# Attention layer of a two-layer decoder: the strided heads' O step six slots later, no weight or x read ahead of the last value rows, token sums in wider steps

## The chip, the cores and the metric

The kernel runs on one core of a Trainium2 chip. The metric is the device time of one execution in microseconds (us); the number given for a kernel is the median of several executions. Beside these times there is one execution taken by the hardware profiler: its time, its span (first to last recorded instruction) and its trace. The trace knows the engines PE (TensorE, matrix products), DVE (VectorE), ACT (ScalarE), POOL (GpSimd), SP (SyncE), and the DMA queues that these engines issue to; in rows of the trace `SPq` is a transfer issued on SP, `POOL ... DMA_DIRECT2D` one issued on POOL.

## What is computed

Two layers over 512 tokens of width 1024, all in float32. Layer 0 mixes tokens with dilated attention (8 output heads of width 128, three groups of heads whose windows and dilations are 128/1, 512/4 and 2048/16); layer 1 with a gated linear recurrence. Each mixer is followed by a convolutional FFN of inner width 3072. Only layer 0's mixer is touched here. Cut to what matters:

```
for layer in range(2):
    h = rms_norm(x, norm_mix_pre[layer])
    h = dilated_attention_mixer(h, w_qkv, w_o, rel_bias)      # layer 0
    x = x + rms_norm(h, norm_mix_post[layer])
    h = rms_norm(x, norm_ffn_pre[layer])
    h = conv_ffn(h, ...)
    x = x + rms_norm(h, norm_ffn_post[layer])

def dilated_attention_mixer(x, w_qkv, w_o, rel_bias):
    qkv = x @ w_qkv                       # 3 groups x (q, k, v) x 8 heads x 128
    for g in range(3):                    # per group: banded softmax attention over t, t-d, t-2d, ...
        o_g, lse_g = dilated_group_attention(q_g, k_g, v_g, bias_g, WINDOWS[g], DILATIONS[g])
    alpha = softmax(stack(lse), axis=0)   # the groups are mixed by their denominators
    return sum(alpha * o) @ w_o
```

## The kernel before

**Precision and weights.** Every operand of a large product is split into a high and a low part (`split`, lines 146 to 148: ACT writes the high part `whi` on L147, DVE the low part `wlo` on L148), and a product is three matmuls: high by high, low by high, high by low. Weights come from DRAM in chunks of 0.5 or 1 MB into `raw` tiles, of which there are `RAW_BUFS = 3`. `pump` (L275 to L309) splits the next piece of a chunk when there is room for it, and then starts chunk reads on SP (`load`, L317) as long as fewer than three are in hand. A read of chunk n+3 therefore waits for the DVE split that empties chunk n, and everything that SP is to issue after it waits too, since an engine works through its program in order.

**The order of the work.** PE's order is written out by slots. `slot(f, 0.25)` runs one piece of matmul work `f` (12 matmuls of a weight chain, or a quarter of a value tile) and then moves all the *sides*, generators that carry the vector work, the small products and the transfers of the heads, on by a quarter of their unit: a `yield 2` in a side is eight slots, a `yield 0.5` two. `later(n, f)` puts a piece n ticks later. There are no priorities at run time: each engine executes its own list in this order and waits on semaphores.

**The attention layer.** First come the 8 heads of the first group with the plain projections (head pairs `hp` 0 to 3, `local`), until about 157 us. At the same time `token_sums` (L818) forms sums and differences of the hidden state's token halves (`B` tiles, then their splits `T`) that the later chains use as operands; it is a side, and its steps were one tile apart in `yield 1`. Then follow four rounds of `ROUND = 44` slots, one for each pair of strided heads. A round holds four chains (queries and keys of the two other groups, L1171, with evictions and combinations on ACT and DVE in L1180 to L1189) and the value rows of the same heads (`value_quarters`, L1107).

**Value rows.** When a value tile of 128 tokens is done, `evict(t)` scales it on ACT (L1145) and writes it on SP to a DRAM array `vrows` (L1146). After the fourth, `by_residue` reads `vrows` back with a token stride of four into four tiles `vp` (L1203, SP), so that the dilated heads find their keys in one tile. In rounds 0 to 2 this is put five ticks after the last eviction; in round 3 right behind it.

**A strided head.** `strided(h)` scores (L1282), exponentiates, and sends the weights of its two groups to DRAM and back turned (`turned` L435, `fetches` L443, both on POOL, four reads to a fetch) into `ft`. It also sends its own mixing weights out and back as `cn` (L1317, L1319). After a pause (`yield 2`) comes the O step: 16 matmuls `O<-ft,vp` (L1348), a DVE product o*cn (L1351) and a DVE sum with the result in PSUM (L1354). The heads of `hp` start when their round's chains are done, so the O step of `hp` 0 falls into round 1, that of `hp` 1 into round 2, that of `hp` 2 into round 3. The last two heads, 6 and 7, come behind round 3 and turn their weights on PE instead (`PT`, L1337).

**Behind the rounds.** `rows_proj` multiplies by w_o (L392, `acc`). `prep(2)` does part of it ahead of the last heads' O step, `prep(4)` and `run` the rest, followed by the post norm (L555), the residual sum with x (L560), the pre norm of the FFN and its first matmuls (L392, `ps`). x has meanwhile lost its place in SBUF to the token sums; `x_again` reads it back in four transfers of 0.5 MB (L803, on POOL), and the two gain vectors are read on SP (L143). The chunks of the FFN's up projection (`raw<-in_ffn_w_up_dram`) are 1 MB each.

Of the kernel before, what the change touches and what calls it, by code (L numbers as in the profile page):

```python
# [81 lines left out]
def kernel(  # L82
# [65 lines left out]
        nc.vector.tensor_tensor(lo, raw, hi.bitcast(F32), op=ALU.subtract)  # L148

    plan = []  # L150
    state = {"dma": 0, "cv": 0, "used": 0, "live": 0, "next": 0, "hold": False, "even": False}
    raws, units, pieces = {}, {}, []
    sides, first_w, first_y, one = [], [], [], []

# [128 lines left out]
    def pump(limit=2):  # L283

        for _ in range(limit):
            if not pieces:
                refill()
            while pieces and pieces[0][0] is None:
                pieces.pop(0)[1]()
            if not pieces or pieces[0][0][0] >= state["dma"]:  # L290
                continue
            if state["live"] + 2 - (pieces[0][0][1] in HALF) <= HALVES:
                key, cuts, last = pieces.pop(0)
                cuts = cuts()
                his, los = [], []
                for n, raw in enumerate(cuts):
                    hi, lo = (
                        wp.tile([P] + list(raw.shape[1:]), F32R, tag=t, name=nm("w" + t)) for t in ("hi", "lo")
                    )
                    split(hi, lo, raw)  # L300
                    his.append(hi)
                    los.append(lo)
                units[key] = (his, los)
                state["live"] += len(cuts)
                state["used"] += last
                while pieces and pieces[0][0] is None:
                    pieces.pop(0)[1]()
            while state["dma"] < len(plan) and state["dma"] - state["used"] < RAW_BUFS:
                load()  # L309

    def load():
# [25 lines left out]
    def side(steps, delay=1):  # L337
        sides.append([delay, steps])
# [460 lines left out]
    def x_again():  # L799

        X[0] = cp.tile([P, 4, D], F32, tag="x_sb", name=nm("x_sb"))
        for t in range(4):
            nc.gpsimd.dma_start(X[0][:, t], x[0, t * P : (t + 1) * P, :])  # L803
        yield 0

    def x_back():

# [3 lines left out]
    def token_sums(hT, T, first=False):  # L811

        if not first:
            assert len(sides) == 1
            d = dp.tile([P, 4, D], F32, name=nm("x_kept"))
            nc.gpsimd.dma_start(d, X[0])
            kept.append(d)
        homes = cp.tile([P, 4, D], F32R, tag="x_sb", name=nm("T"))  # L818
        homes = [homes[:, n] for n in range(4)]
        homes += [cp.tile([P, D], F32R, tag="gain", name=nm("T"), bufs=2) for _ in range(1 if first else 2)]  # L820
        homes = [[h[:, 0:512], h[:, 512:1024]] for h in homes]
        if first:
            homes += [[gen(F32R, "T") for _ in range(2)]]
            homes += [[wp.tile([P, 512], F32R, tag=t, name=nm("T")) for _ in range(2)] for t in ("hi", "lo")]
            state["live"] += 2
        else:
            homes += [[gen(F32R, "T") for _ in range(2)] for _ in range(2)]
        homes = [[h.rearrange("p (k t) -> p k t", k=2) for h in hs] for hs in homes]
        yield 1

        def both(k0, n):
            o = gen(s="B").rearrange("p (k t) -> p k t", k=2)
            hi, lo = (h[:, k0 : k0 + 2, n * 256 : n * 256 + 256] for h in hT)
            tt(o, hi.bitcast(F32), lo.bitcast(F32), op=ALU.add)
            return o

        tt = nc.vector.tensor_tensor

        def negative(o, a, b):
            nc.vector.scalar_tensor_tensor(o, a, -1.0, b, op0=ALU.mult, op1=ALU.subtract)  # L840

        def whole(k0, n):
            return [both(k0 + 2 * k, n) for k in range(2)]

        def parted(n, b):
            for k in range(2):
                split(homes[2 * n][k], homes[2 * n + 1][k], b[k])

        b11, b12 = whole(0, 0), whole(0, 1)
        yield 1  # L850
        for k in range(2):
            tt(b11[k], b11[k], b12[k], op=ALU.subtract)
        parted(0, b11)
        yield 1
        b22 = whole(4, 1)
        for k in range(2):
            if first:
                tt(b12[k], b22[k], b12[k], op=ALU.subtract)
                negative(b22[k], b11[k], b22[k])
            else:  # L860
                tt(b12[k], b12[k], b22[k], op=ALU.subtract)
                tt(b22[k], b22[k], b11[k], op=ALU.add)
        yield 1
        parted(1, b22)
        T.extend([homes[2 * n], homes[2 * n + 1]] for n in range(4))
        yield 1 if first else 8
        parted(2, b12)
        yield 1 if first else 3
        b21 = whole(4, 0)
        yield 1  # L870
        for k in range(2):
            if first:
                negative(b21[k], b22[k], b21[k])
            else:
                tt(b21[k], b21[k], b22[k], op=ALU.subtract)
        yield 1
        parted(3, b21)

    LEFT = {5: ("s1", 1), 1: ("w11", 0), 3: ("s4", 1), 2: ("w12", 0), 6: ("s2", 1), 7: ("s3", 1), 4: ("a22", 1)}
# [104 lines left out]
    def attention(hT, post, pre):  # L984
# [142 lines left out]
        def value_quarters(vs, prep):  # L1127

            vd = dp.tile([S, 512], F32, name=f"vrows{len(vrows)}")
            vrows.append(vd)  # L1130
            ids = [chunk(), chunk()]
            banks = {}

            def quarter(t, u):
                if not u:
                    banks[t] = psum("v")
                products(banks[t], t, u, take(ids[u // 2], u % 2))
                if t == 3:
                    done()
                if u == 3:  # L1140
                    later(1, lambda: evict(t))

            def evict(t):
                o = gen(s="v")
                nc.scalar.activation(o, banks[t], AF.Copy, scale=first_y[0][:, t : t + 1])  # L1145
                nc.sync.dma_start(vd[t * P : (t + 1) * P, :], o)  # L1146
                if t == 3:
                    if prep:
                        by_residue(vd, vs)
                    else:  # L1150
                        later(5, lambda: by_residue(vd, vs))
                elif t == 2 and prep:
                    prep(2)

            order = [(t, u) for t in range(4) for u in range(4)]
            return [lambda t=t, u=u: quarter(t, u) for t, u in (order if prep else sorted(order, key=lambda x: x[1]))]
# [42 lines left out]
        def by_residue(vd, vs):  # L1199

            for r in range(4):
                o = gen(s="vp")
                nc.sync.dma_start(o, vd.rearrange("(u r) c -> r u c", r=4)[r])  # L1203
                vs.append(o)
# [68 lines left out]
        def strided(h, hh, qks, v):  # L1273
# [49 lines left out]
            if h < 6:  # L1323
                for d in ds:
                    pt, reads = fetches(d)
                    for read in reads:
                        read()
                        yield 0.5
                    pts.append(pt)
                yield 2  # L1330
            else:
                yield 1
                for L in Ls:
                    ps = psum("PT")
                    for r in range(4):
                        c = slice(r * P, (r + 1) * P)
                        nc.tensor.transpose(ps[:, c], L[:, c], ident)  # L1337
                    pt = gen(s="PT")
                    nc.scalar.activation(pt, ps, AF.Copy)
                    pts.append(pt.rearrange("p (r c) -> p r c", r=4))  # L1340
                if hh:
                    state["hold"] = False
                yield 4.25 if hh else 4.5
# [56 lines left out]
        for hp in range(4):  # L1400
            pairs, vs = [[[None] * 2 for _ in range(2)] for _ in range(2)], []
            for c in range(4):
                f = chain(right, pairs[c // 2][c % 2], None if c % 2 else SCALE)
                steps.update((ROUND * hp + APART * c + QUAD[p], f(p)) for p in QUAD)

            def heads(hp=hp, pairs=pairs, vs=vs):
                for hh in range(2):
                    side(strided(2 * hp + hh, hh, pairs, vs), 0.25 + 0.25 * hh)
                state["hold"] = True
                if hp == 3:  # L1410
                    side(x_again(), 6.25)

            end = ROUND * hp + max(QUAD.values()) + 3 * APART
            steps[end] = lambda f=steps[end], g=heads: (f(), later(2, g))
            steps.update((ROUND * hp + n, q) for n, q in zip(QUARTERS, value_quarters(vs, prep if hp == 3 else None)))
# [223 lines left out]
```

## Time and profile before

| | us |
|---|---|
| timed runs | 1456.08, 1457.62, 1460.43 |
| median of the timed runs | 1457.62 |
| profiled execution, its time | 1452.73 |
| profiled execution, its span | 1450.9 |
| PE busy in the span | 1426.5 |
| rounds 0 to 3 and the O step of the last heads | about 157 to 476 |

The profiled execution is 4.9 us shorter than the median of the timed ones; sums made on the trace stand against its own time. PE is the engine to read first: it is busy for 98% of the span, so time is won only where PE stands still or runs at a lower clock. In the trace's windows a column gives the clock that was granted to PE (1.00 is full speed, 0.50 half), another the share of the core's DMA engines in use (values a little over 1 occur).

### The profile page before, as it was taken

Reading aid. Unit: us, or ns where it says so; the run is one execution under the profiler, and the core shown is the slowest. Engines: PE = TensorE matmul, PEld = TensorE weight load, DVE = VectorE, ACT = ScalarE, POOL = GpSimd, SP = SyncE. Lnnn points to the kernel's source line nnn. Section 1 sums busy time; section 2 is a strip of 40 time slices with the busy share of each in tenths; the row PEclk is TensorE's granted clock in tenths of the full one; section 3 lists DMA queues with packets and bytes.
Section 4 is the critical chain, followed back from the end, with each engine's and each line's share of the span. In section 5 each row is a group of like instructions: output and inputs, shape, how many; then the busy total and the mean of one; then the engine's idle time right before and its main releaser. Section 6 shows DMA issues by size and latency. Waiting matters only on the chain.

```text
span 1450.9 us, 21582 instructions
## 1 busy us (share of the span) xinstructions
PE 1426.5 (98%) x8021; PEld 1250.4 (86%) x8021; DVE 1023.0 (71%) x2017; ACT 723.1 (50%) x1486; POOL 178.3 (12%) x313
## 2 busy tenths in 40 slices
PE   9999999999998999999999999999999999999998
PEld 7888999898986898899988888988898999988886
DVE  6685898786855789977774338868789977774333
ACT  7353556363635455555553334489564555553231
POOL 0241333030301100111000001000100111000000
PEclk9999999999999999999999999999999999999999
DMA  7553456464655535645453232441435645453201
GB/s 223 158 160 114 124 162 176 141 184 133 169 184 157 173 97 155 149 110 123 130 198 116 87 102 73 126 136 58 124 91 161 155 106 143 124 189 116 88 1 59
DMA packets 143266, 191.30 MB, mean 132 GB/s; under 512 B 9344, under 2 KB 119384, under 8 KB 142648
## 3 DMA queue, kind: packets, MB, share of 16 engines
q1 hardware_dynamic: 114280, 145.48, 31.4%
q0 software_dynamic: 28032, 43.39, 12.9%
q8 instruction: 63, 1.03, 0.3%
q10 hardware_dynamic: 848, 1.05, 0.2%
q14 instruction: 43, 0.35, 0.1%
HBM read 170.93 MB, written 18.96 MB: 131 GB/s over the span
## 4 chain that ended last, share of the span: by engine, by line
PE 63%; ACT 4%; DMA 3%; DVE 3%; issue 1%; POOL 0%; DVEq 0%; POOLq 0%; ACTq 0%; SPq 0%
PE ps L392 25%; PE acc L392 23%; PE ps L934 11%; PE v L1107 1%; DVE xb L1442 1%; PE ps L1171 1%; DMA vrows<-v 1%; ACT whi L147 1%; DVE wlo L148 1%; DMA crow<-s 1%; PE O L1348 1%; ACT sig L1463 1%; PE tr L482 1%; DMA ft<-turned 0%; ACT sig L1482 0%
## 5 line engine op out<-in xcount | busy, mean ns | idle before, releaser
L148 DVE TENSOR_TENSOR wlo<-raw,whi 128x512 fp32r<-128x512 f32 x600 | 395.7, 686 | 201.4 <-ACT whi L147 200.6
L147 ACT ACTIVATE whi<-raw 128x512 fp32r<-128x512 f32 x600 | 358.9, 627 | 312.1 <-PE acc L392 118.2
L392 PE MATMUL ps<-hT,whi 128*128 128x512 f32 (+1 forms) x1728 | 486.0, 367 | 0.0
L392 PEld LDWEIGHTS ps<-hT,whi 128*128 128x128 f32 x1728 | 308.2, 189 | 48.8
L392 PE MATMUL ps<-hT,wlo 128*128 128x512 f32 (+1 forms) x864 | 316.0, 366 | 0.0
L392 PE MATMUL acc<-whi,ahi 128*128 128x512 f32 x512 | 199.6, 390 | 0.0
L392 PE MATMUL acc<-whi,alo 128*128 128x512 f32 x512 | 199.4, 389 | 0.1
L392 PE MATMUL acc<-wlo,ahi 128*128 128x512 f32 x512 | 199.2, 389 | 0.0
L392 PEld LDWEIGHTS ps<-hT,wlo 128*128 128x128 f32 x864 | 163.0, 189 | 27.0
L753 DVE SCALAR_TENSOR_TENSOR u<-ps,cols,u 128x511 f32<-128x511 f32 x192 | 143.6, 748 | 49.0 <-ACT u L749 45.6
L749 ACT ACTIVATE u<-ps,cols 128x512 f32<-128x512 f32 x96 | 73.9, 770 | 82.6 <-DVE ps L949 42.0
L392 PEld LDWEIGHTS acc<-whi,alo 128*128 128x128 f32 x512 | 96.1, 188 | 20.3 <-DVE alo L148 0.5
L392 PEld LDWEIGHTS acc<-wlo,ahi 128*128 128x128 f32 x512 | 96.1, 188 | 20.0
L392 PEld LDWEIGHTS acc<-whi,ahi 128*128 128x128 f32 x512 | 96.1, 188 | 19.8
L1107 PE MATMUL v<-whi,hT 128*128 128x512 f32 x320 | 106.6, 396 | 0.0
L1171 PE MATMUL ps<-T,whi 128*128 128x256 f32 x512 | 93.2, 282 | 1.1 <-DVE ps L1189 1.1
L934 PE MATMUL ps<-T,whi 128*128 128x256 f32 x512 | 92.8, 280 | 0.0
L184 POOL DMA_DIRECT2D raw<-in_ffn_w_up_dram x32 | 41.4, 1453 | 361.8 <-DVE wlo L148 223.6
L1171 PEld LDWEIGHTS ps<-T,whi 128*128 128x128 f32 x512 | 79.7, 189 | 2.6 <-DVE ps L1189 1.6
L934 PEld LDWEIGHTS ps<-T,whi 128*128 128x128 f32 x512 | 80.1, 189 | 1.6
L443 POOL DMA_DIRECT2D ft<-turned x136 | 74.5, 555 | 32.0 <-issue 11.3
L1171 PE MATMUL ps<-hT,whi 128*128 128x256 f32 x384 | 72.2, 287 | 0.0
(212 smaller groups left out, 2021.6 us busy)
## 6 DMA issues: line engine op xcount, KB each, us to landing
raw<-in_ffn_w_up_dram SPq DMA_DIRECT2D x48, 1024.0 KB
raw<-in_attn_w_qkv_dram SPq DMA_DIRECT2D x67, 512.0 KB
raw<-in_ffn_w_down_dram SPq DMA_DIRECT2D x24, 1024.0 KB
raw<-in_ffn_w_up_dram POOLq DMA_DIRECT2D x32, 256.0 KB, 4.7
raw<-in_lru_w_in_dram SPq DMA_DIRECT2D x8, 1024.0 KB
turned<-T POOLq DMA_DIRECT2D x26, 256.0 KB, 3.2
ft<-turned POOLq DMA_DIRECT2D x104, 64.0 KB, 4.4
vrows<-v SPq DMA_DIRECT2D x16, 256.0 KB
```

The lines of the kernel that those rows point to most:

```text
L147: nc.scalar.activation(hi, raw, AF.Copy)
L148: nc.vector.tensor_tensor(lo, raw, hi.bitcast(F32), op=ALU.subtract)
L184: nc.gpsimd.dma_start(to, src, accum_op=ALU.add)
L392: mm(dst, l[a], r[b], start=start and n == 0, stop=stop and n == 2)
L443: nc.gpsimd.dma_start(t[32 * c : 32 * c + 32].rearrange("j (b x) -> j b x", b=4), d.rearrange("(b j) (c x) -> c j b x", j=32, c=4)[c],)
L482: nc.tensor.transpose(ps[:, k * P : (k + 1) * P], xs[i][:, k * P : (k + 1) * P], ident)
L749: nc.scalar.activation(u, ps, AF.Identity, scale=cc[:, j : j + 1], bias=cc[:, 48 + j : 49 + j])
L753: nc.vector.scalar_tensor_tensor(u[:, d:], ps[:, : S - d], wc, u[:, d:], op0=ALU.mult, op1=ALU.add)
L934: mm(y[b][:, 0:256], W[wa][0][:, k, :], right[n](ha, k), start=n in (1, 5) and k == q == 0, stop=k == 3 and q == 2, skip_group_check=True,)
L1107: mm(bank, hT[a][:, k, t * P : (t + 1) * P], W[b][k % 2][:, 0, :], start=(k, a, b) == (0, 0, 0), stop=(k, a, b) == (KD - 1, 1, 0),)
L1171: mm(dst, W[wa][0][:, k, :], right[n](ha, k), start=n in (1, 5) and k == q == 0, stop=k == 3 and q == 2, skip_group_check=True,)
L1348: mm(po[:, c], vtile(v, r, 2 * gi + hh), pts[gi][:, r], start=gi == 0, stop=gi == 1)
```

## The change

1. In `strided`, for heads 0 to 5, the pause ahead of the O step is 3.5 units instead of 2: six slots.
2. A flag `quiet` is set when the heads of the last round start. While it is set, `pump` starts no chunk read. It is cleared behind the issue of the last `by_residue`. `x_again` no longer starts on POOL 6.25 units after the heads, but on SP right behind these reads, one transfer for each unit.
3. In the first `token_sums` each `yield 1` is a `yield 2`.

```diff
-    state = {..., "hold": False, "even": False}
+    state = {..., "hold": False, "even": False, "quiet": False}
...
-            while state["dma"] < len(plan) and state["dma"] - state["used"] < RAW_BUFS:
+            while not state["quiet"] and state["dma"] < len(plan) and state["dma"] - state["used"] < RAW_BUFS:
                 load()
...
         for t in range(4):
-            nc.gpsimd.dma_start(X[0][:, t], x[0, t * P : (t + 1) * P, :])
-        yield 0
+            nc.sync.dma_start(X[0][:, t], x[0, t * P : (t + 1) * P, :])
+            yield 1
...
     def token_sums(hT, T, first=False):
...
-        yield 1
+        yield 1 + first
...
-        yield 1 if first else 8
+        yield 2 if first else 8
         parted(2, b12)
-        yield 1 if first else 3
+        yield 2 if first else 3
...
                 if t == 3:
                     if prep:
                         by_residue(vd, vs)
+                        state["quiet"] = False
+                        side(x_again())
...
                         read()
                         yield 0.5
                     pts.append(pt)
-                yield 2
+                yield 3.5
...
                 state["hold"] = True
-                if hp == 3:
-                    side(x_again(), 6.25)
+                state["quiet"] = hp == 3
```

How it moves instructions is seen best in the engines' lists. SP's list at the last value rows, before (`vrows` is the write of a value tile, `vp` the read back, `raw<-in_ffn_w_up_dram` an FFN chunk of 1 MB):

```order
L1146 DMA vrows_1672<-v_5184 128x512
L317 DMA raw_5243<-in_ffn_w_up_dram 128x8x256
L1146 DMA vrows_1672<-v_5259 128x512
L1203 DMA vp_5262<-vrows_1672 128x512
L1203 DMA vp_5264<-vrows_1672 128x512
L1203 DMA vp_5266<-vrows_1672 128x512
L1203 DMA vp_5268<-vrows_1672 128x512
L317 DMA raw_5278<-in_ffn_w_up_dram 128x8x256
L143 DMA gain_5288<-in_norm_mix_post_dram 128x1024
L143 DMA gain_5290<-in_norm_ffn_pre_dram 128x1024
L317 DMA raw_5340<-in_ffn_w_up_dram 128x8x256
```

and the same place in the changed kernel (its line numbers are shifted by up to 2):

```order
L1146 DMA vrows_1672<-v_5184 128x512
L1146 DMA vrows_1672<-v_5257 128x512
L1205 DMA vp_5260<-vrows_1672 128x512
L1205 DMA vp_5262<-vrows_1672 128x512
L1205 DMA vp_5264<-vrows_1672 128x512
L1205 DMA vp_5266<-vrows_1672 128x512
L317 DMA raw_5276<-in_ffn_w_up_dram 128x8x256
L317 DMA raw_5278<-in_ffn_w_up_dram 128x8x256
L143 DMA gain_5288<-in_norm_mix_post_dram 128x1024
L143 DMA gain_5290<-in_norm_ffn_pre_dram 128x1024
L803 DMA x_sb_5312<-in_x_dram 128x1024 x2
L317 DMA raw_5343<-in_ffn_w_up_dram 128x8x256
```

The first FFN chunk stood ahead of the fourth value row's write and now stands behind the four `vp` reads, next to the second chunk; two of the x reads follow the gains, the other two the third chunk. On POOL the four x reads stood behind the last `cn` and are gone:

```order
L1319 DMA cn_5169<-crow_5167 128x512
L803 DMA x_sb_5396<-in_x_dram 128x1024 x4
L435 DMA turned_5491<-T_5489 128x512
L435 DMA turned_5495<-T_5493 128x512
L443 DMA ft_5497<-turned_5491 32x4x128 x4
```

DVE's list around the O step of `hp` 0, in round 1, before (`o` is a head's output, L1351 the product with cn, L1354 the sum with O; L1184 and L1189 are sums of a chain that PE's later steps wait for; `wlo` are splits of weights):

```order
L1351 TENSOR_TENSOR o_1007<-o_1007,cn_2604 128x512
L148 TENSOR_TENSOR wlo_3073<-raw_2775,whi_3072 128x512
L148 TENSOR_TENSOR wlo_3077<-raw_2775,whi_3076 128x512
L1030 SCALAR_TENSOR_TENSOR qk_3095<-ps_2812,roots 128x512
L1354 TENSOR_TENSOR o_1007<-O_3062,o_1007 128x4x128
L1351 TENSOR_TENSOR o_1141<-o_1141,cn_2635 128x512
L1184 TENSOR_TENSOR ps_2999<-ps_2999,part_2969 128x512
L1030 SCALAR_TENSOR_TENSOR qk_3124<-ps_2999,roots 128x512
L1354 TENSOR_TENSOR o_1141<-O_3098,o_1141 128x4x128
```

and in the changed kernel (L1353 and L1356 are the old L1351 and L1354; L1186 and L1191 the old L1184 and L1189; L229 to L241 combine weights of the next chain):

```order
L1191 TENSOR_TENSOR ps_2956<-ps_2956,part_2970 128x256
L148 TENSOR_TENSOR wlo_3141<-raw_2908,whi_3140 128x512
L148 TENSOR_TENSOR wlo_3145<-raw_2908,whi_3144 128x512
L148 TENSOR_TENSOR wlo_3165<-raw_3034,whi_3164 128x512
L229 TENSOR_TENSOR raw_3034<-raw_3034 128x4x128
L1353 TENSOR_TENSOR o_993<-o_993,cn_2604 128x512
L148 TENSOR_TENSOR wlo_3192<-raw_3034,whi_3191 128x512
L233 TENSOR_TENSOR raw_3034<-raw_3034 128x4x128
L1356 TENSOR_TENSOR o_993<-O_3181,o_993 128x4x128
L1353 TENSOR_TENSOR o_1127<-o_1127,cn_2635 128x512
L148 TENSOR_TENSOR wlo_3221<-raw_3034,whi_3220 128x512
L1030 SCALAR_TENSOR_TENSOR qk_3236<-ps_2956,roots 128x512
```

The two heads' four operations moved behind the sums L1184 and L1189 that they stood around, in among the weight combinations of the next chain. PE's O matmuls moved by six chain steps with them; the list of PE is otherwise the same.

More of the change, by code (lines that the diff above doesn't have):

```diff
@@ L150 @@
     plan = []
-    state = {"dma": 0, "cv": 0, "used": 0, "live": 0, "next": 0, "hold": False, "even": False}
+    state = {"dma": 0, "cv": 0, "used": 0, "live": 0, "next": 0, "hold": False, "even": False, "quiet": False}
     raws, units, pieces = {}, {}, []
@@ L849, in token_sums @@
         b11, b12 = whole(0, 0), whole(0, 1)
-        yield 1
+        yield 1 + first
         for k in range(2):
@@ L853, in token_sums @@
         parted(0, b11)
-        yield 1
+        yield 1 + first
         b22 = whole(4, 1)
@@ L862, in token_sums @@
                 tt(b22[k], b22[k], b11[k], op=ALU.add)
-        yield 1
+        yield 1 + first
         parted(1, b22)
         T.extend([homes[2 * n], homes[2 * n + 1]] for n in range(4))
-        yield 1 if first else 8
+        yield 2 if first else 8
         parted(2, b12)
-        yield 1 if first else 3
+        yield 2 if first else 3
         b21 = whole(4, 0)
-        yield 1
+        yield 1 + first
         for k in range(2):
@@ L875, in token_sums @@
                 tt(b21[k], b21[k], b22[k], op=ALU.subtract)
-        yield 1
+        yield 1 + first
         parted(3, b21)
```

## The prediction

> **What bounds the kernel now.** I read the head of the page and its first part, then the waits of PE. The rows of the waits are engine, tile, line, releaser: sum in us, times, longest.
>
> ```profile
> span 1450.9 us, 21582 instructions
> PE 1426.5 (98%) x8021; PEld 1250.4 (86%) x8021; DVE 1023.0 (71%) x2017; ACT 723.1 (50%) x1486; POOL 178.3 (12%) x313
> PE O L1348 <- DMA vp<-vrows: 6.9, 2, 6.7
> PE O L1348 <- DMA ft<-turned: 5.4, 2, 3.2
> PE O L1348 <- DMA toe<-rowv: 1.8, 1, 1.8
> PE warm L1558 <- DVE one L1603: 1.5, 1, 1.5
> PE ps L1171 <- DVE ps L1189: 1.1, 1, 1.1
> PE O L392 <- DVE plo L1259: 0.6, 1, 0.6
> ```
>
> PE is idle for 1450.9 − 1426.5 = 24.4 us. The first three rows, 14.1 us, are all O matmuls of strided heads that wait for a transfer. So the O step is what a change can win here, and nothing else holds more than 1.5 us. PE's timeline has the single places (start, duration, in brackets the idle time before):
>
> ```profile
> 261.19 1.35 PE L1348 MATMUL O<-ft,vp 128*128 128x128 f32 x10 [2.15 <-DMA ft<-turned]
> 262.75 0.71 PE L1348 MATMUL O<-ft,vp 128*128 128x128 f32 x4 [0.21 <-DMA vp<-vrows]
> 334.14 2.43 PE L1348 MATMUL O<-ft,vp 128*128 128x128 f32 x14 [3.23 <-DMA ft<-turned]
> 340.46 0.48 PE L1171 MATMUL ps<-hT,whi 128*128 128x256 f32 x2
> 406.98 1.88 PE L1348 MATMUL O<-ft,vp 128*128 128x128 f32 x14 [1.84 <-DMA toe<-rowv]
> 411.84 0.48 PE L1171 MATMUL ps<-hT,whi 128*128 128x256 f32 x2
> 469.78 6.59 PE L1348 MATMUL O<-PT,vp 128*128 128x128 f32 x32 [6.69 <-DMA vp<-vrows]
> 410.29 1.79 PE O L1348 x16
> ```
>
> (The last row is from the chain of waits.) Head pair 0 waits 2.15 + 0.21 = 2.36, pair 1 3.23, pair 2 1.84, pair 3 6.69. Behind the two longer waits PE is also slow, as its windows show (time, busy, clock granted, DMA share, GB/s):
>
> ```profile
> 336.00:338.00 2.00, 2.00 (x11) 0.50 1.09 337
> 408.00:410.00 2.00, 2.00 (x19) 1.00 0.99 395
> 472.00:474.00 2.00, 2.00 (x10) 0.50 1.05 345
> ```
>
> The clock is halved behind the waits of 3.23 and 6.69 us, and full behind that of 1.84. The price: from 334.14 to 340.46, 6.32 us, PE does the 14 + 12 + 16 matmuls that take 411.84 − 406.98 = 4.86 at full clock, so 1.46 in pair 1. The last pair's 32 O matmuls take 6.59 instead of 2 × 1.79 = 3.58, so 3.01.
>
> **The change part by part.** *The O step six slots later, pairs 0 to 2.* It lets six chain steps, 72 matmuls, pass ahead of the O matmuls. Twelve take
>
> ```profile
> 408.86 1.44 PE ps L1171 x12
> ```
>
> so the O step comes 6 × 1.44 = 8.6 us later. The transfers it waits for do not move: their places in POOL's and SP's lists are the same relative to the chains. They were late by at most 2.36 (first wait and the small one behind it), 3.23 and 1.84; a later O step overshoots these by 5.4 or more. Removed: 2.36 + 3.23 + 1.46 + 1.84 = 8.9 us. The work that fills the gap is the chain that came behind before, so PE's total is the same.
>
> What it adds lies on DVE: two products (L1351) and two sums (L1354) per round move in among the next chain's combinations, and PE's fourth step of that chain waits for L1189.
>
> ```profile
> 257.54 0.69 DVE L1351 TENSOR_TENSOR o<-o,cn 128x512 f32<-128x512 f32 x1
> 263.50 1.10 DVE L1354 TENSOR_TENSOR o<-O,o 128x512 f32<-128x512 f32 x1 [2.81 <-PE O L1348]
> 269.57 0.43 DVE L1189 TENSOR_TENSOR ps<-ps,part 128x256 f32<-128x256 f32 x1 [0.18 <-PE ps L1171]
> 282.57 0.43 DVE L1189 TENSOR_TENSOR ps<-ps,part 128x256 f32<-128x256 f32 x1
> 283.42 0.40 PE L1171 MATMUL ps<-T,whi 128*128 128x256 f32 x2
> ```
>
> The four cost 2 × 0.69 + 2 × 1.10 = 3.58 us. L1189 ends at 283.00, and PE takes it at 283.42: 0.42 to spare, and no idle time of DVE is recorded ahead of it. If all four came on top, PE would wait 3.58 − 0.42 = 3.2 in each of three rounds. But 32 O matmuls, 2 × 1.79 = 3.58 on PE, move to the same place and put off PE's need by as much; and DVE, freed of its own wait of 2.81 at 263.50, comes there earlier. At their present place the same four ran ahead of the L1189 at 269.57, which still waited 0.18 for PE. I take 0, with 0 to 3.2 a round kept for the range; no gain, since only one wait of this kind, 1.1, is left anywhere.
>
> *The last value rows.* SP's timeline, one row of POOL's, a row of the page's DMA issues (KB each, median us from issue to landing) and one of the windows:
>
> ```profile
> 453.37 0.38 SPq L317 DMA_DIRECT2D raw<-in_ffn_w_up_dram  x1
> 454.18 0.32 SPq L1146 DMA_DIRECT2D vrows<-v  x1
> 466.63 1.75 SPq L1203 DMA_DIRECT2D vp<-vrows  x4
> 452.96 2.10 POOL L803 DMA_DIRECT2D x_sb<-in_x_dram  x4
> turned<-T POOLq DMA_DIRECT2D x26, 256.0 KB, 3.2
> 459.00:460.00 1.00, 1.00 1.08 424
> ```
>
> The fourth write (0.25 MB) is issued at 454.18 and its reader starts at 466.63, 12.45 later. It shares the DMA engines with an FFN chunk (1 MB) issued 0.8 before it and four x reads (2 MB) issued 1.2 before; the window at 459 is full. Other writes of the same 256 KB to DRAM, `turned<-T`, land after 3.2 in the median. With the chunk and x behind it, only the last `cn` (0.25 MB) is beside it, 0.6 us at 424 GB/s. I take 3.2 + 0.6 = 3.8. The `vp` reads start near 458.0 and the first O matmul 469.78 − 466.63 = 3.15 behind that, 461.1. PE's work ahead of O ends at 469.78 − 6.69 = 463.09. So the wait of 6.69 goes, with 2.0 to spare, and with it the 3.01 of half clock: 9.7 us. The upper bound of the write's time is its present 12.45 (nothing won), the lower 3.2.
>
> What now comes late is what was moved behind: FFN chunks 0 and 1, the gains, x. Their uses, all to come 9.7 earlier on this clock:
>
> ```profile
> 484.02 0.69 DVE L555 TENSOR_TENSOR post<-acc,gain 128x512 f32<-128x512 f32 x1 [5.09 <-ACT junk L399]
> 486.70 1.41 DVE L560 SCALAR_TENSOR_TENSOR x_sb<-post,s,x_sb 128x512 f32<-128x512 f32 x2
> 489.11 2.18 ACT L147 ACTIVATE whi<-raw 128x512 fp32r<-128x512 f32 x4
> 466.00:472.00 6.00, 0.69 0.66 201
> ```
>
> That is 474.3 for the gain, 477.0 for x, 479.4 for the first split of chunk 0. From 458.0 on SP issues vp (1 MB), two chunks (2 MB), gains (1 MB), the first two x reads (1 MB): 5 MB. At the 424 GB/s of a full window that is 12 us, 470; at the 201 of the slowest window here (466 to 472) 25 us, 483. The rows of full windows above are 337 to 424, so I take 15 at most, 473: hidden behind the 27 us of w_o matmuls that follow O. Cost 0, up to 6 if the slow rate held.
>
> The Trainium skill ("DMA: Bandwidth & Descriptors", "Queues, rings and completion order") speaks against this part: each DMA engine serves its queues in turn, so on a queue of its own x would get a share at once, while on SP's it stands behind everything issued before. By that rule x lands later than on a queue of its own, which favours the slower rival below, while the sum, made with x behind 4 MB as it is, stays 18.6. The trace agrees so far that the write at 454.18 took long beside the x reads of POOL's queue.
>
> *Token sums.* Their DVE work moves from 55 to 102 us into a stretch twice as long.
>
> ```profile
> L834 DVE TENSOR_TENSOR B<-hT,hT x8: 679/682/685, 55.1 to 84.2; 128x512 f32<-128x512 f32 x8
> L148 DVE TENSOR_TENSOR T<-B,T x8: 681/684/694, 60.7 to 101.8; 128x512 fp32r<-128x512 f32 x8
> 60.00:100.00 40.00, 39.43 (x189) 32.84 (x187) 34.61 (x91) 22.26 (x54) 13.93 (x26) 1.00 0.52 149
> 100.00:145.00 45.00, 45.00 (x213) 37.67 (x212) 27.35 (x71) 16.08 (x39) 11.23 (x21) 1.00 0.37 113
> 85.51 0.39 PE L392 MATMUL O<-plo,vhi 128*128 128x256 f32 x1 [0.57 <-DVE plo L1259]
> ```
>
> (In the windows the third busy time is DVE's.) DVE is busy for 34.61 of 40 us where the sums stand and 27.35 of 45 where they go: cover enough. They may end the one wait of 0.57 for `plo` here, or put a pair of 0.68 us operations ahead of some other `plo` (1.4). I take 0, from −0.6 to +1.5.
>
> **The sum.** 8.9 + 9.7 = 18.6. The profiled execution took 1452.73, so 1434.1 by the trace; carried to the median of the timed runs, which is 4.9 above it, 1457.62 − 18.6 = 1439.0.
>
> One term hangs on the clock. The Trainium skill ("TensorE: Matmul & The Clock Gate", "Part 1: The HAM clock gate") gives the halved clock after at least one idle window of about 3.4 us. By that rule the wait of 3.23 would not be followed by it, the 1.46 would not be there, and the time would be 1440.5; the window at 336 shows 0.50, so here the row decides.
>
> **The rivals.** *DVE takes the place of the transfers.* In rounds 1 to 3 the four operations hold L1189 up. For it: DVE's 0.42 to spare and no gap of its own there. Against: PE's O work moves along. Price about two thirds of the bound, 2.1 a round, 6.4: 1445.4. *The fourth write stays slow.* If its 12.45 are its own latency or the cn's and not the load beside it, pair 3 keeps 9.7: 1448.7, or half of that, 1443.9. For it: two ends 10 us apart. Against: the median of the `turned` writes. *Slower: x at the end of SP's queue.* x has left a queue where it was issued at 452.96 for one where 4 MB stand ahead. Past 477.0 each us is an idle PE at the first FFN matmuls. For a loss x must be late by more than the 18.6 won, landing after 495.6, so 5 MB in 37.6 us or 133 GB/s. The slowest window here, 201, gives 483, 6 late, so two thirds of the gain would survive. It needs SP to be held by something else, such as the third chunk's wait for a raw buffer in front of the last two x reads; at 10 us past the point, 1457.6 + 10 = 1467.6. *The change does nothing*, since the waits follow the O step or have another cause than I think: 1457.6.
>
> **How the numbers follow.** Forecast 74%, DVE 12%, write still slow 8%, x late 4%, nothing 2%. The likeliest case has 1434 to 1444: three small DVE waits or two or three us of x late above, below it the spread of the timed runs (4.4 us) and a wait that I have not counted. The range reaches to 1447 to take in the rival of DVE and half of the slow write: 1433 to 1447. This kernel's measurement tells a change from none at about 0.3%, 4.4 us. Faster by more than that are the forecast and the next two rivals, 94%, less a little for mixtures: 0.93. Within it 0.03, slower 0.04.
>
> **What would show it.** Right: no O row in PE's waits, clock 1.00 in every window of the rounds, the fourth `vrows` landing within 4 us of its issue, O of pair 3 in 3.6 us, PE idle near 10 us. DVE's rival: a row `ps <- ps` of 2 us or more, three times. The slow write: O still waiting for `vp`. x late: a DVE L560 that waits for x and a gap of PE ahead of its first FFN matmuls. The forecast is wrong if the span falls by less than 12 us or if the freed time returns in the FFN.

## The result and the profile after

The changed kernel takes 1431.9 us in the median of five runs (1431.64 to 1433.13), against 1457.62 for the kernel before in its five (1454.97 to 1460.43): a ratio of 0.9823, 95% interval 0.9806 to 0.9841, or 25.8 us less (23.2 to 28.3). The forecast was 1439.0 with a range from 1433 to 1447. The sign and the places were right, the size too small, and the time lies 1.1 us below the range. Later runs beside the experiments gave the kernel before medians of 1454.97 (23 runs), 1455.03 (27) and 1454.96 (9), so about 23 us of the 25.8 are the change and the rest is that its first five runs were long ones.

The changed kernel's profiled execution took 1431.89, its span 1430.1. All waits of PE that the view lists (engine, tile, line, releaser: sum, times, longest; lines are shifted by 1 or 2; the row of `tr` is the first load of x at the start of the kernel, not the reads that were moved):

```profile
PE warm L1559 <- DVE one L1604: 1.5, 1, 1.5
PE ps L1173 <- DVE ps L1191: 0.8, 1, 0.8
PE tr L493 <- DMA x_sb<-in_x_dram: 0.3, 1, 0.3
```

Every O row is gone. PE's timeline shows the O steps with no idle time ahead of them (of pair 0 both heads, of pairs 1 and 2 the first, then the last heads):

```profile
266.37 1.95 PE L1350 MATMUL O<-ft,vp 128*128 128x128 f32 x16
269.59 1.95 PE L1350 MATMUL O<-ft,vp 128*128 128x128 f32 x16
...
335.40 1.95 PE L1350 MATMUL O<-ft,vp 128*128 128x128 f32 x16
...
404.44 1.95 PE L1350 MATMUL O<-ft,vp 128*128 128x128 f32 x16
...
451.91 3.73 PE L1350 MATMUL O<-PT,vp 128*128 128x128 f32 x32
```

The last one takes 3.73 instead of 6.59, so at full clock; and the windows around all four (time, PE busy, clock, DMA share, GB/s) have no halved clock and no gap:

```profile
250.00:280.00 30.00, 30.00 (x235) 1.00 0.69 199
320.00:350.00 30.00, 30.00 (x235) 1.00 0.66 186
395.00:425.00 30.00, 30.00 (x218) 1.00 0.53 177
445.00:490.00 45.00, 45.00 (x225) 1.00 0.69 234
```

SP's timeline at the last value rows:

```profile
445.30 1.75 SPq L1205 DMA_DIRECT2D vp<-vrows  x4
447.10 1.05 SPq L317 DMA_DIRECT2D raw<-in_ffn_w_up_dram  x2
448.19 3.63 SPq L143 DMA_DIRECT2D gain<-in_norm_mix_post_dram  x1
451.86 0.43 SPq L143 DMA_DIRECT2D gain<-in_norm_ffn_pre_dram  x1
452.33 0.91 SPq L803 DMA_DIRECT2D x_sb<-in_x_dram  x2
453.34 0.38 SPq L317 DMA_DIRECT2D raw<-in_ffn_w_up_dram  x1
453.76 6.08 SPq L803 DMA_DIRECT2D x_sb<-in_x_dram  x2
```

The fourth value tile leaves ACT at 443.1 (442.44 and 0.69 in ACT's timeline, not quoted), its write is issued at 443.15 (SP's timeline in a narrower window, not quoted), and the reads of it start at 445.30: 2.15 us from the issue of the write to its reader, where it was 12.45. The chain of waits, which before went through this write and read, now goes through PE alone:

```profile
452.07 3.57 PE O L1350 x32
455.64 27.22 PE acc L392 x120
```

**What each pair cost.** A good ruler, that is a mark that returns in every round, is the first score matmul (tile S) of each round, since all rounds hold the same work. Tile S before, one row for each round (duration min/median/max in ns, first and last start):

```profile
L1282 PE MATMUL S<-qk,qk x32: 270/275/276, 215.7 to 221.9; 128*128 128x128 f32 x32
L1282 PE MATMUL S<-qk,qk x32: 270/275/276, 287.6 to 293.8; 128*128 128x128 f32 x32
L1282 PE MATMUL S<-qk,qk x32: 270/275/275, 361.6 to 367.8; 128*128 128x128 f32 x32
L1282 PE MATMUL S<-qk,qk x32: 270/275/275, 433.0 to 439.2; 128*128 128x128 f32 x32
```

and after:

```profile
L1284 PE MATMUL S<-qk,qk x32: 270/275/275, 214.9 to 221.1; 128*128 128x128 f32 x32
L1284 PE MATMUL S<-qk,qk x32: 270/275/275, 283.9 to 290.1; 128*128 128x128 f32 x32
L1284 PE MATMUL S<-qk,qk x32: 270/275/275, 352.9 to 359.2; 128*128 128x128 f32 x32
L1284 PE MATMUL S<-qk,qk x32: 270/275/275, 422.0 to 428.2; 128*128 128x128 f32 x32
```

From round to round it is 71.9, 74.0 and 71.4 us before, 69.0, 69.0 and 69.1 after. So pair 0 cost 2.9, pair 1 5.0, pair 2 2.3. Behind that, from the first score of round 3 to the first w_o matmul behind the last O step, it is 476.38 − 433.0 = 43.4 before and 455.64 − 422.0 = 33.6 after, 9.7 or so. The remaining 0.8 is ahead of round 0. Sum 20.7; the spans are 1450.9 − 1430.1 = 20.8 apart. The 0.8 need not be the change: the first score of round 0 starts between 214.2 and 215.9 in the profiles of all runs below, at 214.9 in a second profile of the kernel before.

A finer ruler shows where in the round the 10.2 sit. The O matmuls before (the rows of each pair that the prediction does not show):

```profile
258.65 0.39 PE L1348 MATMUL O<-ft,vp 128*128 128x128 f32 x2
264.73 1.95 PE L1348 MATMUL O<-ft,vp 128*128 128x128 f32 x16
330.53 0.39 PE L1348 MATMUL O<-ft,vp 128*128 128x128 f32 x2
338.76 1.95 PE L1348 MATMUL O<-ft,vp 128*128 128x128 f32 x16
404.68 0.46 PE L1348 MATMUL O<-ft,vp 128*128 128x128 f32 x2
410.13 1.95 PE L1348 MATMUL O<-ft,vp 128*128 128x128 f32 x16
```

From the first O matmul of a pair's first head to that of its second head it is 6.08, 8.23 and 5.45 us before, and 3.22, 3.23 and 3.22 after. The differences, 2.86, 5.00 and 2.23, sum to 10.1: practically all that the pairs cost lies there.

### The profile page after: what moved, and what is told of

It is laid out like the page before. It is cut to its first block, busy times and chain, and to the rows that moved or that the text cites. A ratio compares the mean times of both kernels' runs of the same rounds, so it can differ in the third digit from the quotient of the medians.

```text
span 1430.1 us, 21591 instructions
## 1 busy us (share of the span) xinstructions
PE 1420.4 (99%) x8021; PEld 1246.0 (87%) x8021; DVE 1022.3 (71%) x2017; ACT 723.2 (51%) x1486; POOL 176.2 (12%) x309
## 4 chain that ended last, share of the span: by engine, by line
PE 91%; ACT 4%; DVE 4%; DMA 1%; issue 1%; POOL 0%; DVEq 0%; SPq 0%; ACTq 0%
PE ps L392 32%; PE acc L392 24%; PE ps L934 11%; PE ps L1173 10%; PE v L1107 7%; PE v L1045 1%; DVE xb L1443 1%; DVE wlo L148 1%; PE O L1350 1%; PE S L1284 1%; PE S L1232 1%; ACT whi L147 1%; ACT sig L1464 1%; PE tr L482 1%; PE O L392 0%
## 5 line engine op out<-in xcount | busy, mean ns | idle before, releaser
L1173 PE MATMUL ps<-T,wlo 128*128 128x256 f32 x256 | 72.0, 281 | 0.0
```

The costliest lines, as they stand in the source:

```text
L1173: mm(dst, W[wa][0][:, k, :], right[n](ha, k), start=n in (1, 5) and k == q == 0, stop=k == 3 and q == 2, skip_group_check=True,)
```

## The experiments

Each ran beside the kernel before on the same chip. The ratio of the times is given with its 95% interval, and the us saved are that ratio times the median of the kernel before. It is not the quotient of the two medians; the plain differences of the medians are up to 1.6 us larger (14.6, 9.4, 0.1, 4.4, 6.7, 14.3 and 3.9 for the runs from the O step alone to PE kept warm), and all of them lie inside the intervals given.

**The kernel before again.** No edit.

> The kernel before, unchanged, to see how its executions differ. Its profiled execution took 1452.73 and its five timed ones 1454.97 to 1460.43, while those of the changed kernel lie within 1.5 us. Theory A: the difference between executions sits in the same waits for transfers at the O steps, and in the halved clock behind them; then executions lie between 1452 and 1461, the longer ones have the lower granted clock (0.001 of the clock is 1.45 us of work), and a profile of a longer one shows the extra time at rounds 1 to 3 and the last heads alone. Theory B: it is a matter of the chip or of where the kernel was loaded, the same for all kernels; then the executions differ by as much here as in the next three kernels, and the clock does not follow the time.

Measured: 1454.45 in the median of 12 runs, 1452.19 to 1458.32; ratio 1.0001 (0.9988 to 1.0014). Over these 12 and the 23 runs beside them the time rises by 1.18 us for each 0.001 that the mean clock falls (correlation −0.88), from 1448 at 0.997 to 1458.8 at 0.990. The profiled execution, of 1452.90:

```profile
PE O L1348 <- DMA ft<-turned: 9.5, 4, 3.7
PE O L1348 <- DMA vp<-vrows: 5.9, 1, 5.9
```

Pairs 0 to 2 waited 9.5 here, 7.4 in the execution of the prediction. So executions of one kernel do differ at the O steps; whether by the clock or by the landings (the times at which the transfers arrive) was left to a later run. Theory B's sign, a clock that does not follow the time, is not there.

**The parts alone.** The O step:

```diff
-                yield 2
+                yield 3.5
```

> Only the pause ahead of the O step, 3.5 for 2. If the waits of pairs 0 to 2 are hidden whole: PE's waits for ft and toe are gone, that for vp of the last heads (6.7) stays, and the span is 10.2 below the kernel before (the two traces of before and after give 2.9 + 5.0 + 2.3 for the three pairs; my prediction had 8.9), near 1440.7. If the four DVE operations take the place of the transfers, a row ps <- ps of 2 us or more comes up three times and the gain is 4. Theory A: the executions still differ by some us, since the wait of the last heads is left, and the median lies up to 4.9 above the profiled one. Theory B: the median lies 4.9 above whatever the part.

Measured: 1440.39 (1439.64 to 1443.89), ratio 0.9911 (0.9894 to 0.9929), or 13.0 us less (10.3 to 15.4). PE's waits:

```profile
PE O L1348 <- DMA vp<-vrows: 5.4, 1, 5.4
PE warm L1558 <- DVE one L1603: 1.5, 1, 1.5
PE ps L1171 <- DVE ps L1189: 0.7, 1, 0.7
```

The wait of the last heads is left, all other O waits are gone, and no new wait for DVE came up (the row `ps <- ps` read 1.1 before). My 8.9 for this part lies below the interval.

The last value rows:

```diff
-            while state["dma"] < len(plan) and ...
+            while not state["quiet"] and state["dma"] < len(plan) and ...
...
-            nc.gpsimd.dma_start(X[0][:, t], x[0, t * P : (t + 1) * P, :])
-        yield 0
+            nc.sync.dma_start(X[0][:, t], x[0, t * P : (t + 1) * P, :])
+            yield 1
...
                         by_residue(vd, vs)
+                        state["quiet"] = False
+                        side(x_again())
...
-                if hp == 3:
-                    side(x_again(), 6.25)
+                state["quiet"] = hp == 3
```

> Only the second part: no weight read ahead of the last value rows, x behind them on SP. Expected: the last heads' wait of 6.7 and the half clock behind it go, 9.7 us, span near 1441.2; pairs 0 to 2 wait as before (ft 5.4, toe 1.8). If the load beside the fourth write was not the cause, the wait stays and the span is 1450. Theory A: the sum of the medians' gains of this, the O step and the token sums is the 25.7 of the whole change, of which about 5 that the traces of single executions do not show are shared between this and the O step.

Measured: 1445.62 (1443.66 to 1447.0), ratio 0.9941 (0.9923 to 0.9960), 8.6 us less (5.8 to 11.2). The forecast's 9.7 is inside. Its profile has the waits of pairs 0 to 2 and none of the last heads (the O step reads `ft` and `vp` alone; `toe` is a table for the scores that POOL also reads in, and its name in these rows is the profile's inference):

```profile
PE O L1350 <- DMA toe<-rowv: 4.7, 2, 2.8
PE O L1350 <- DMA ft<-turned: 3.0, 1, 3.0
```

and in this execution all three pairs ran at half clock for a while (the windows that read 1.00, 0.94, 1.00 before):

```profile
250.00:280.00 30.00, 27.22 (x212) 0.94 0.66 194
320.00:350.00 30.00, 26.96 (x206) 0.89 0.68 193
395.00:425.00 30.00, 28.04 (x224) 0.94 0.70 217
```

The token sums:

```diff
     def token_sums(hT, T, first=False):
-        yield 1
+        yield 1 + first
...
-        yield 1 if first else 8
+        yield 2 if first else 8
...
-        yield 1 if first else 3
+        yield 2 if first else 3
```

> Only the token sums in wider steps. The traces of before and after stand 0.6 apart from the plo wait on and 0.8 from the first scores of round 0; so a gain of 0.6 to 0.8 in the span at most, 1450.1, which the spread of the timed runs hides. If the sums' DVE work now holds up a later plo, a new wait of up to 1.4 and no gain. All the waits at the O steps stay; by theory A the timed runs spread as those of the kernel before.

Measured: 1454.86 (1449.02 to 1456.75), ratio 0.9999 (0.9986 to 1.0013): nothing. The three parts alone sum to 13.0 + 8.6 + 0.1 = 21.7 by the ratios, 24.1 by the medians; the whole was 23 against the usual median before, so the parts add up within their intervals.

**The halves of the second part.** First only the flag, with x on POOL as before:

```diff
+                state["quiet"] = hp == 3
                 if hp == 3:
                     side(x_again(), 6.25)
```

> No weight read ahead of the last value rows, but x stays on POOL, issued about 1.2 us ahead of the fourth write. Everything else as before, so pairs 0 to 2 wait as before. With both moved the write and its reads were 3.5 us early for the last O step (vp issued at 445.3, O at 451.9, 3.1 to land). If transfers share by turns between the two queues, the write shares with 2 MB of x and lands perhaps 2 to 3 us later, and the vp reads too: the last wait falls from 5.5 to 6.7 to 0 to 3, no half clock behind it, gain 6 to 9.7 of the second part's 9.4. If x, issued first, is served first (2 MB at 400 GB/s, 5 us), the wait is 2 to 4 and half clock follows in some executions: gain 3 to 6. If the FFN chunk ahead on the same queue is not what held the write up, gain 0.

Measured: 1450.63 (1446.75 to 1456.72), ratio 0.9975 (0.9961 to 0.9989), 3.6 us less (1.6 to 5.7). The last O step in its timeline:

```profile
465.65 1.44 PE L1349 MATMUL O<-PT,vp 128*128 128x128 f32 x8 [1.93 <-DMA vp<-vrows]
467.89 0.71 PE L1349 MATMUL O<-PT,vp 128*128 128x128 f32 x4 [0.80 <-DMA vp<-vrows]
469.03 2.50 PE L1349 MATMUL O<-PT,vp 128*128 128x128 f32 x20 [0.42 <-DMA vp<-vrows]
```

It waits for one `vp` after the other, 3.2 in all. Of the cases named ahead of the run this fits the second, wait 2 to 4 and gain 3 to 6. Then only x, with the chunk ahead of the write:

```diff
                         by_residue(vd, vs)
+                        side(x_again())
...
-                if hp == 3:
-                    side(x_again(), 6.25)
```

(with the same two lines for SP in `x_again`).

> x behind the last value rows on SP, but the first FFN chunk stays ahead of the fourth write on SP's own queue. Pairs 0 to 2 as before. 1 MB ahead in the same queue at 400 GB/s is 2.6 us, so the write lands 2.6 later than with both moved, inside the 3.5 to spare: gain about 9, the whole of the second part, which makes holding the chunk back a needless half. If the chunk is the cause and not x, the wait of 5 to 7 stays and the gain is 0 to 2.

Measured: 1448.37 (1445.25 to 1452.73), ratio 0.9961 (0.9946 to 0.9976), 5.7 us less (3.5 to 7.9). In its profile:

```profile
463.07 1.42 PE L1349 MATMUL O<-PT,vp 128*128 128x128 f32 x8 [0.17 <-DMA vp<-vrows]
465.00 0.71 PE L1349 MATMUL O<-PT,vp 128*128 128x128 f32 x4 [0.51 <-DMA vp<-vrows]
466.48 2.50 PE L1349 MATMUL O<-PT,vp 128*128 128x128 f32 x20 [0.77 <-DMA vp<-vrows]
```

1.45 is left. From the issue of the fourth write to its reader (SP's timelines) it took 12.45 us before, 7.58 with the flag only (454.81 to 462.39), 5.94 with x only (453.99 to 459.93), 2.15 with both: the chunk alone adds 3.8, not the 2.6 that I expected, and x alone 5.4. So both loads, the chunk ahead on the same queue and x on the other, hold up the write and its reads; each half wins a part (x alone less than the 9 that I expected), and the two halves' 3.6 and 5.7 add up to the 8.6 of both within their intervals.

**How much later.** Half the distance, three slots:

```diff
-                yield 2
+                yield 2.75
```

> A pause of 2.75: the O step of heads 0 to 5 three slots later, 4.3 us, half of the change's. The waits of pairs 0 to 2 in the five profiles with the old place are 1.8 to 3.7 us (0.8 + 2.2 in one case), so a later start of 4.3 covers them all with 0.5 to 2 to spare: 14 us gained as with six slots, O rows gone. If the transfers' landing moves with PE (they share DMA with weights that a faster PE asks for sooner) waits of 1 to 2 us are left and the gain is 8 to 12.

Measured: 1440.71 (1440.44 to 1441.73), ratio 0.9908 (0.9892 to 0.9923), 13.4 us less (11.2 to 15.7): the same as six slots. The landings do not run away with PE.

**PE kept warm.** In the kernel before, ahead of the O matmuls of the first head of each pair, without a use for the result:

```diff
             po = psum("O")
+            for _ in range({0: 9, 2: 12, 4: 8, 6: 23}.get(h, 0)):
+                mm(po, hT[0][:, 0, :P], hT[0][:, 0, :], start=True, stop=True)
             for r in range(4):
```

> The kernel before, with matmuls of no use (high part of the hidden state, 128 x 512, into the bank that the O step then starts anew) put into PE's list just ahead of the O matmuls of the first head of each pair: 9, 12, 8 and 23, at 0.227 us each 2.0, 2.7, 1.8 and 5.2 us, which is a little less than PE stands still there. No transfer moves. Theory A (what differs between executions, and the part of the gain that the waits do not hold, is the halved clock behind the waits): the waits shrink in the record but the O steps start when they did; the clock is 0.998 to 0.999 in all executions, the time falls by 1.18 us for each 0.001 of clock from 0.9937, so by 5 to 7 us to 1448, and the executions lie within some 3 us. Theory B (executions differ in when the transfers land): 1454 as before, spread 10 us, whatever the clock does. Extra matmuls that come out longer than the wait would add at most 1 us.

Measured: 1451.16 (1448.18 to 1455.80), ratio 0.9976 (0.9963 to 0.9989), 3.5 us less (1.6 to 5.4). The clock is 0.999 in nine of the 12 executions, and these lie within 3.3 us (1448.18 to 1451.52); in the other three it is 0.996 to 0.998, and they are the longest (1454.40 to 1455.80). The profiled one is of these: PE waited 2.10 for pair 2 behind the extra matmuls, and the window from 395 to 425 reads 0.94, so PE was not kept warm there. Theory A does not hold in its strong form: the clock is up by 0.0054 in the mean, which would be 7.9 us if all of it were time in which PE works, but the time is down by less than half of that. Theory B of this run, that the landings differ between executions, is needed for what is left: the two long ones at 0.998 are 4.1 and 5.5 us longer than the median of the nine, and 0.001 of the clock is 1.5 us. The 3.5 is what a warm clock wins with the transfers where they are; what the extra matmuls cost where the transfers land early is in it and was not measured apart. In its last O step (a longer execution, 1454.40) PE, at full clock, waits for the single reads that it was too slow to wait for before:

```profile
465.48 5.38 PE L1346 MATMUL O<-hT 128*128 128x512 f32 x23
471.48 0.71 PE L1350 MATMUL O<-PT,vp 128*128 128x128 f32 x4 [0.62 <-DMA vp<-vrows]
472.60 1.48 PE L1350 MATMUL O<-PT,vp 128*128 128x128 f32 x8 [0.41 <-DMA vp<-vrows]
475.54 2.50 PE L1350 MATMUL O<-PT,vp 128*128 128x128 f32 x20 [1.47 <-DMA vp<-vrows]
```

From the end of the useful work to the end of O it is 478.0 − 465.5 = 12.5 us here, 476.4 − 463.1 = 13.3 before.

**The parts together.** The changed kernel without its third part:

```diff
-        yield 1 + first
+        yield 1
```

(and so on for all steps of the token sums)

> The changed kernel with the token sums back in steps of one tile. Alone they gave 0 (0.9999, within 0.13%). If the parts add up, this is the changed kernel's 1431.9 within 1 us, with the 0.6 of the plo wait back at most, and all executions within 2 us and the clock at 0.998 to 0.999, since no O wait is left that could differ. If the token sums matter only once the O waits are gone (a wait hidden behind another), it is 2 us or more longer, 1434.

Measured: 1431.64 (1431.33 to 1432.33), ratio 0.9836 (0.9822 to 0.9849). And the changed kernel with three slots:

```diff
-                yield 3.5
+                yield 2.75
```

> The changed kernel with a pause of 2.75 instead of 3.5, so three slots later than before instead of six. By the run with three slots alone the waits of pairs 0 to 2 (at most 3.7) are covered by 4.3 us: 1432 with six slots or three, no O row in PE's waits. If three slots leave less to spare than the landings differ between executions, some of the executions are 1 to 4 us longer and have a lower clock.

Measured: 1431.98 (1431.54 to 1432.97), ratio 0.9837 (0.9824 to 0.9851). Both equal the changed kernel within 0.3 us. The executions of the changed kernel and of these two (five, five and four), whose profiles have no wait at an O step, lie within 1.5 us for each kernel. With that the first run's theory B falls, by which executions differ whatever the kernel does.

**The pairs in all profiles with the old place of the O step**, in us over 69.0:

| kernel | pair 0 | pair 1 | pair 2 | sum |
|---|---|---|---|---|
| before | 2.9 | 5.0 | 2.4 | 10.3 |
| before again | 3.0 | 5.5 | 3.7 | 12.2 |
| last value rows | 4.6 | 6.0 | 3.8 | 14.4 |
| token sums | 3.2 | 5.0 | 6.2 | 14.4 |
| flag only | 4.9 | 5.3 | 2.2 | 12.4 |
| x only | 4.4 | 5.2 | 1.9 | 11.5 |

The mean is 12.5, which agrees with the 13.0 and 13.4 that six and three slots won. The execution that I worked from has the smallest sum. Where profiles differ, they differ at such places: the execution of the token sums is 2.9 us longer than that of the kernel before, with 4.1 more at the pairs, 0.5 less from the last scores to the end of the last O step, and 0.6 less ahead of round 0.

## Why the prediction was too small

**What bounds the kernel, and where the time goes: right.** All O waits went, nothing came in their place, PE's idle time is 1430.1 − 1420.4 = 9.7 (I had said near 10).

**Pair 3: right in size.** 9.7 forecast, 9.7 between the traces, 8.6 (5.8 to 11.2) alone. I was too careful with the write: 3.8 estimated, 2.15 in the trace. And one detail was wrong: I counted 3.01 of the 9.7 to the halved clock. The warm run shows that at full clock PE would have waited for the `vp` reads during much of it. The sum holds because the reads became early as well.

**DVE in place of the transfers: did not happen.** The four operations were priced at 0 to 3.2 a round and taken as 0. After, L1191 of that chain in round 1 stands at

```profile
277.96 0.43 DVE L1191 TENSOR_TENSOR ps<-ps,part 128x256 f32<-128x256 f32 x1
```

and PE takes it at 279.89 (a row of the chain of waits), so 1.5 us to spare, where 0.42 were before: PE's own O work moved along, as argued. PE's one wait for such a sum in the rounds is the 0.8 of the list above, 1.1 before. **x late: did not happen.** L560 followed L555 and the small operations of the norm with no wait for a transfer:

```profile
463.27 0.69 DVE L555 TENSOR_TENSOR post<-acc,gain 128x512 f32<-128x512 f32 x1 [5.09 <-ACT junk L399]
465.95 1.42 DVE L560 SCALAR_TENSOR_TENSOR x_sb<-post,s,x_sb 128x512 f32<-128x512 f32 x2
```

**Token sums: right, 0.** The `plo` wait of 0.57 is missing in the changed kernel with the old token sums too (PE's waits there are the 1.5 for `one` and 0.6 for `ps`), and in the second profile of the kernel before, so it was an accident of one execution.

**The step that failed** is the first term of the sum, "Removed: 2.36 + 3.23 + 1.46 + 1.84 = 8.9 us" for pairs 0 to 2, together with the sentence that carried the sum to the median "which is 4.9 above it". The term measured 10.1 between the two traces and 13.0 (10.3 to 15.4) in the run of the O step alone, and of the offset nothing was left. The forecast missed by 7.1: 2.2 since the two traces stand 20.8 apart and not 18.6, and 4.9 since the changed kernel's median is its profiled execution's time, with no 4.9 on top. Of the 2.2, 1.2 to 1.3 are pairs 0 to 2: they cost 10.1 between the O matmuls and 10.2 by the rounds, not 8.9. What the rows of waits leave out is this. Sixteen O matmuls at full clock take 1.71 from their start to the start of what follows (410.13 to 411.84), 0.107 each, but the matmuls ahead of a wait are drawn longer (the first two of a pair 0.39 to 0.46 instead of 0.21), and the idle time in brackets begins only at that drawn end; so each of the four rows of waits is 0.2 to 0.3 short, 0.9 in all. The other 0.3 is twice 0.15: the 14 matmuls behind pair 2's wait took 1.63 from start to start (406.98 to 408.61) and not the 1.49 of full clock, a cost that I left out, and as the price of 1.46 in pair 1 was taken against pair 2's 4.86, it is too small by the same. The remainder of the 2.2, about 0.8, is ahead of round 0 and differs between executions. Of the 4.9, 2.7 are the first three timed runs (1457.62 against 1454.97 over 23 runs), and 2.2 are real: the profiled execution was a short one, with the smallest cost of the pairs of six. Waits for transfers and the halved clock behind them were where executions differ, and I had treated the offset between the profile and the median as something that a change leaves alone. The part of it that was real belonged to the very waits that the change removes. A term of 12.5 from several profiles, against the usual median of 1455, gives 1455 − 12.5 − 9.7 = 1432.8; both figures come from runs made after the prediction.

**Left open:** why the landings differ between executions by some us. The DMA share is at its full value at each of these places (0.99 to 1.09 in the windows behind pairs 1 to 3 that the prediction shows), but no run took the weight reads away from rounds 1 to 3. How the saving of the pairs splits into wait and clock is also settled only roughly: 3.5 (1.6 to 5.4) of both parts' 23 came with the clock alone.

## What to carry to other kernels

A wait for a transfer is not one number: its length differs between executions of the same kernel, so take it from several profiles, and look whether timed runs spread and whether the granted clock follows the time. If they do, the offset between the profile and the median goes away with the wait. And take the median from more than three runs: 2.7 of the 4.9 came from that alone. The idle time that a profile puts ahead of a matmul can be short by some tenths, so measure a stop from start to start too. A consumer that waits for a round trip through DRAM can sometimes be moved behind independent work of its own engine; here that cost nothing, and three slots did what six did, and a read that nobody needs yet is better issued behind the one that somebody waits for.

## What was unexpected of the hardware

The halved clock does not follow the length of the wait. Behind waits of pair 0 it came after 2.59 us ("x only", 0.94 in the window from 250) and not after 2.87 ("token sums", 1.00); behind pair 2 it came after 1.96 ("last value rows") and not after 2.15 behind 0.82 ("before again"). Every wait of 2.99 us or more at pairs 0 to 2 was followed by it, in all profiles of the table. The Trainium skill ("TensorE: Matmul & The Clock Gate", "Part 1: The HAM clock gate") says that the window in which idleness is counted runs free of the program, which fits that it comes and goes; its figure of about 3.4 us of idleness does not fit 1.96, which is 2.35 from start to start.

SP stood 3.63 us at the issue of a gain read and 6.08 at two x reads (its timeline above), with 3 MB issued in the 3 us ahead of the first and 6 MB in the 8.5 us ahead of the second. Before, with less behind each other, an issue of a gain took 0.43 to 0.58. The first gain took 3.80 in the flag-only run too, which has the same two chunks ahead of it, and 0.64 in the x-only run, which has one. That the bytes outstanding are the cause is still only my reading. Nothing waited for it here.
